# A room of its own for gathered token rows, and more filler products, in a two-layer mixture-of-experts encoder on Trainium2

## The chip, the cores and the metric

The kernel runs on 1 core of one Trainium2 chip, as one launch. The metric is the device time of one execution in microseconds (us); the time of the kernel before is the median of 3 runs.

## What is computed

Two layers, each an attention block and an expert block, over 512 tokens of width 1024, in float32. Here only the expert block matters ("expert choice": each of 16 experts takes the 64 tokens that like it best):

```python
h = rmsnorm(x, ffn_norm_g)
affinity = softmax(h @ w_router)                  # 512 x 16
gate, idx = top_k(affinity.T, 64)                 # per expert
xe = h[idx]                                       # 16 x 64 x 1024
a, u = xe @ w_gate, xe @ w_up                     # 1024 x 1408 per expert
y = (silu(a) * u) @ w_down                        # 1408 x 1024 per expert
x = x + scatter_add(y * gate, idx)
```

The weights of the experts are read once from HBM: 192 chunks of 1408 KB a layer.

## The kernel before, in words

A layer of `body` runs as attention (split by hand into units and placed by a table of due times), the output product with the router (the function `attention` returns the products, and the loop after it interleaves them with the router's work), and the expert block.

**Expert block.** The experts are taken in 8 pairs p = 0 to 7. Per pair there are 24 chunks of weights, numbered n = 24p + 8s + k: s = 0 is `w_gate`, s = 1 `w_up`, s = 2 `w_down`, and k is the slice of 128 rows. TensorE (PE) does the products of a chunk with the pair's 2 x 64 tokens (`L1302` for gate and up, 12 records a chunk; `L1347` for down, 14 a chunk on average), then the chunk's room is free. Between up and down stand SiLU on ScalarE (ACT, `L1327`), the product with up on VectorE (DVE, `L1328`) and PE transposes of the result (`L1336`).

**Rooms for chunks.** `load` and `bring` issue the chunk transfers on SyncE's (SP's) queue, in the order of n, and SP stands at each until its room is free. The first 17 chunks (table `ISSUE`) are brought in during attention, into rooms x0 to x11, y0, y1, "apart", the room of the hidden values ("hx") and a shared room "rows". Chunks 17 to 31 go into rooms that the table `AGAIN` names: x0 to x9 (17 to 26, once chunks 0 to 9 are used), y0, y1, x10, x11 (27 to 30, once 11, 12, 14, 15 are used), and x0 a second time (31, once 17 is used). From 32 on, two chunks go at once into a double room, in the order `DOUBLES = "bcdegfa"`: a is x0 and x1, b is x2 and x3, and so on to f; g is y0 and y1. So 32 and 33 wait in b for chunks 19 and 20.

**Rows of the tokens.** For pair p + 1 the 128 token rows are gathered from DRAM by an indirect DMA on GpSimd (POOL, `fetch_rows`, `L1248`), scaled by ACT (`L1249`) and transposed by PE (`L1256`) between up and down of pair p. They land in the room "rows", which for p = 0 first holds chunk 10. So the gather for pair 1 is issued behind chunk 10's products (`ROWS_AT = 2`: up, k = 2); all later ones behind gate's k = 6 (`MARK_AT`), as soon as `marks` has made the row numbers. ACT's instructions run in order: `L1249` stands ahead of the pair's SiLU.

**Router of the last token tile.** `stats`, `add_up`, `settle` and `best` make logits (`L958`), softmax (`L971` to `L977`), a transpose (`L981`), and eight rounds of maximum and replacement on DVE (`L1008`, `L1010`) for tile 3; then the threshold's transpose (`L1082`), ranks (`L1089` to `L1094`), and the first gathered tokens as products with a one-hot matrix (`L1205`), on which chunk 0's products wait. `warm` (`L998`) puts products of x with itself on PE there, whose results nobody reads: `WARM_A` (one 256 wide) before `stats`, `WARM_C` (two of 512) after `settle`, one of 512 in round 4 of `best(2)`, `WARM_P` (one of 512) before the first `L1205`. The scheduler may set them between other products.

`dynamic_dma_scratch_size=4096` reserves bytes of each partition for the descriptors of DMAs that POOL issues.

Of the kernel before, what the change touches and what calls it, by code (L numbers as in the profile page):

```python
# [11 lines left out]
F32 = mybir.dt.float32  # L12
# [17 lines left out]
FF = 1408  # L30
NJ = FF // P
CAP = 64
SLOT = 3072
RING = 3
ISSUE = [(16, "apart"), (0, "x0"), (1, "x1"), (4, "x4"), (11, "y0"), (2, "x2"), (3, "x3"), (10, "rows"), (5, "x5"), (6, "x6"), (7, "x7"), (9, "x9"), (8, "x8"), (13, "hx"), (14, "x10"), (15, "x11"), (12, "y1")]
AGAIN = ["x0", "x1", "x2", "x3", "x4", "x5", "x6", "x7", "x8", "x9", "y0", "y1", "x10", "x11", "x0"]
SINGLES = 32
DOUBLES = "bcdegfa"
GAP = 512
# [24 lines left out]
HALF_AT = 3  # L64
ROWS_AT = 2
END_ON = 'avavaa'
# [74 lines left out]
def body(ctx, tc, x_in, x_t, pos, w_in, w_uq, w_ukv, w_out, w_gate, w_up, w_down, gatt, gfin, params, consts, band, sel, out):  # L141
# [733 lines left out]
    for l in range(L):  # L875
        with ExitStack() as es:
# [196 lines left out]
            stats(t)  # L1073
            add_up(t)
            settle(t)
            warm(WARM_C)
# [20 lines left out]
            nc.vector.tensor_tensor(code, both[:, :, 0, :], both[:, :, 1, :], op=ALU.add)  # L1097
        with tc.tile_pool(name=f"fs{l}", bufs=1, reuse_waits="tile") as fs, tc.tile_pool(name=f"fw{l}", bufs=2, side="right", reuse_waits="tile") as fw, ExitStack() as late:
            early = ExitStack()
# [5 lines left out]

            def shared():

                return fs.tile([P, SLOT], F32, tag="rows", name=nm("shared"))

            def single(tag):  # L1110
                return fx.tile([P, 2 * FF], F32, tag=tag, name=nm("xslot"))

# [20 lines left out]

            near = {tag: single(tag) for tag in ("y0", "y1")}
            fx.tile([P, GAP], F32, tag="gap", name=nm("gap"))
            near.update({f"x{i}": single(f"x{i}") for i in range(12)})
            rooms = {}
            for n, tag in ISSUE:
                bring(n, xb.tile([P, 2 * FF], F32, tag="apart", name=nm("apart")) if tag == "apart" else wide() if tag == "hx" else shared()[:, : 2 * FF] if tag == "rows" else near[tag])

# [3 lines left out]
            def load(n):  # L1144

                if n not in kept:
                    if n < SINGLES:
                        bring(n, single(AGAIN[n - len(ISSUE)]))
                    else:
                        if n == SINGLES:  # L1150
                            early.close()
                            rooms["far"] = late.enter_context(tc.tile_pool(name=f"fd{l}", bufs=1, reuse_waits="tile"))
                            rooms["g"] = double("g")
                            rooms["far"].tile([P, GAP], F32, tag="gap", name=nm("gap"))
                            rooms.update({q: double(q) for q in "abcdef"})
# [86 lines left out]
            def fetch_rows(p):  # L1242

                if p > 0:
                    v, src = shared()[:, :D], xrow_d[l][:, :]
                else:
                    v, src = fw.tile([P, S], F32R, tag="oh", bufs=3, name=nm("rows")).bitcast(F32), xrow_d[l].rearrange("t (h d) -> (t h) d", h=2)
                nc.gpsimd.indirect_dma_start(v, None, src, bass.IndirectOffsetOnAxis(token[:, p : p + 1], 0))  # L1248
                nc.scalar.activation(v, v, AF.Copy, scale=scales[:, p : p + 1])  # L1249
                return v  # L1250
# [41 lines left out]
            for p in range(8):  # L1292
                acc, whole = [], {}
                ahead = [] if p < 7 else [(t, h) for t in range(NT - 1) for h in range(2)] if l == L - 1 else [(t, h) for h in range(2) for t in range(NT)][:6]
                for s, w in enumerate((w_gate, w_up)):
                    bs = [bank() for _ in cuts]
                    acc.append(bs)
                    for k in range(KD):
# [18 lines left out]
                        if w is w_gate and k == MARK_AT and p < 7:  # L1317
                            ohs[p + 1] = marks(p + 1)
                            if p > 0:
                                rows = fetch_rows(p + 1)  # L1320
                        if w is w_up and k == ROWS_AT and p == 0:
                            rows = fetch_rows(1)
                hx = wide()
# [164 lines left out]
```

## Time and profile before

| | |
|---|---|
| median of 3 runs (lowest, highest) | 1909.98 us (1909.73, 1911.14) |
| the profiled execution: its time, its span | 1910.87 us, 1909.1 us |
| PE, DVE, ACT, POOL busy | 1722.2 (90%), 703.6, 428.6, 206.1 us |
| mean granted TensorE clock | 0.981 |
| moved by DMA | 649.28 MB, mean 340 GB/s |
| chain that ended last | PE 48%, DMA 37%, DVE 9%, ACT 3% |

The profile cuts the span into 40 slices of 47.7 us; the expert block of layer 0 is slices 7 to 20, that of layer 1 slices 27 to 40. A granted clock of 1.00 is 2.4 GHz, 0.50 is 1.2 GHz. In a timeline row the first number is the start, the second the time from the first start to the last end of the instructions merged in it; in brackets stand the idle time before and what ended it.

### The profile page before, as it was taken

The page shows a single profiled execution, that of the slowest core. Times are in us where ns is not written, and L with a number is a line of the kernel's source. Part 1 is how long each engine was busy: PE and PEld are TensorE (multiplying, and loading weights), DVE is VectorE, ACT ScalarE, POOL GpSimd, SP SyncE. Part 2 cuts the span into 40 slices and gives each one's busy share as a digit, 9 for nine tenths or more (in the row PEclk, how much of TensorE's full clock was granted, in tenths as well). Part 3 has the DMA queues.
Part 4 walks back from the last instruction along what each step waited for, and adds up shares of the span by engine and source line. Part 5 has one row for each costly group of instructions (what it writes and reads, how often), then busy time and mean ns, then how long its engine had stood idle before and what let it go on. Part 6 is the DMA issues. An engine that isn't in the chain of part 4 may idle for free.

```text
span 1909.1 us, 21766 instructions
## 1 busy us (share of the span) xinstructions
PE 1722.2 (90%) x8798; PEld 895.9 (47%) x8798; DVE 703.6 (37%) x1470; ACT 428.6 (22%) x884; POOL 206.1 (11%) x232
## 2 busy tenths in 40 slices
PE   8999999999987878888899999989998878888887
PEld 6785675344332333333377756743443333333333
DVE  7868856111211112111188698541121112111112
ACT  5347941101000100000043589211100100000101
POOL 1324421000000000000023153210000000000000
PEclk9999998999999999999999999989999999999999
DMA  7874649989999999999948744798999999999996
GB/s 274 248 199 72 163 149 365 396 351 429 429 428 431 428 430 429 429 428 429 397 131 267 170 101 110 246 363 352 409 429 428 430 429 429 429 429 428 430 427 264
DMA packets 82579, 649.28 MB, mean 340 GB/s; under 512 B 8656, under 2 KB 25808, under 8 KB 53040
## 3 DMA queue, kind: packets, MB, share of 16 engines
q1 hardware_dynamic: 68288, 608.43, 78.7%
q0 software_dynamic: 12128, 35.54, 7.9%
q10 hardware_dynamic: 2064, 3.93, 0.6%
q8 instruction: 69, 1.13, 0.2%
q14 instruction: 30, 0.25, 0.0%
HBM read 619.17 MB, written 27.39 MB: 339 GB/s over the span
## 4 chain that ended last, share of the span: by engine, by line
PE 48%; DMA 37%; DVE 9%; ACT 3%; issue 1%; POOL 1%; SPq 0%; DVEq 0%; ACTq 0%; POOLq 0%
PE ps L1302 16%; DMA dslot<-in_w_up_dram 13%; DMA dslot<-in_w_gate_dram 13%; DMA dslot<-in_w_down_dram 9%; PE ps L1347 7%; PE ps L753 6%; PE ps L854 5%; PE ps L762 2%; PE ps L672 2%; PE ps L1277 2%; PE ps L655 2%; DVE sm L604 1%; PE ps L515 1%; ACT P L611 1%; DMA shared<-xrow_d,slots 1%
## 5 line engine op out<-in xcount | busy, mean ns | idle before, releaser
L1302 PE MATMUL ps<-dslot,xe 128*64 128x506 f32 (+1 forms) x2496 | 528.7, 575 | 87.3 <-DMA dslot<-in_w_up_dram 51.7
L1302 PEld LDWEIGHTS ps<-dslot,xe 128*64 128x64 f32 x2496 | 178.3, 139 | 425.8 <-issue 321.3
L1347 PE MATMUL ps<-dslot,hx 128*64 128x512 f32 (+3 forms) x1568 | 275.8, 504 | 46.1 <-DMA dslot<-in_w_down_dram 41.6
L1347 PEld LDWEIGHTS ps<-dslot,hx 128*64 128x64 f32 x1568 | 104.5, 137 | 209.4 <-issue 136.9
L1328 DVE TENSOR_TENSOR hx<-ps,hx 128x506 f32<-128x506 f32 (+1 forms) x48 | 43.4, 968 | 428.7 <-PE ps L1302 383.7
L1269 DVE SCALAR_TENSOR_TENSOR hx<-ps,gates,hx 128x512 fp32r<-128x512 f32 x32 | 22.5, 746 | 363.3 <-ACT hx L1268 363.3
L1268 ACT ACTIVATE hx<-ps,gates 128x512 fp32r<-128x512 f32 x32 | 20.3, 684 | 605.1 <-PE ps L1347 605.1
L753 PE MATMUL ps<-xh,w 128*128 128x512 f32 (+1 forms) x448 | 145.8, 405 | 3.1 <-ACT xh L363 1.4
L1279 DVE TENSOR_TENSOR x<-ps,x 128x512 f32<-128x512 f32 x112 | 69.5, 683 | 184.1 <-PE ps L1277 184.1
L1249 ACT ACTIVATE shared<-shared,slots 128x1024 f32<-128x1024 f32 x14 | 16.1, 1148 | 488.5 <-DMA shared<-xrow_d,slots 455.3
L611 ACT ACTIVATE P<-ps,sm 128x512 f32<-128x512 f32 x168 | 116.5, 704 | 32.1 <-DVE sm L604 30.8
L1248 POOL DMA_INDIRECT shared<-xrow_d,slots x14 | 13.2, 943 | 945.6 <-DVE oh L1239 887.6
L1302 PE MATMUL ps<-xslot,xe 128*64 128x506 f32 (+1 forms) x528 | 109.4, 560 | 3.9 <-DVE xe L1208 2.3
L753 PEld LDWEIGHTS ps<-xh,w 128*128 128x128 f32 (+1 forms) x448 | 84.2, 189 | 28.0 <-ACT xh L363 3.9
L753 PE MATMUL ps<-xl,w 128*128 128x512 f32 (+1 forms) x224 | 85.7, 393 | 0.0
L604 DVE TENSOR_REDUCE sm<-ps 128x1 f32<-128x512 f32 x120 | 78.7, 679 | 5.5 <-PE ps L589 4.6
L655 PE MATMUL ps<-ident,P 128*128 128x128 f32 x512 | 77.5, 274 | 2.0 <-ACT P L611 1.8
L663 ACT COPY pt<-ps 128x512 f32<-128x512 f32 x118 | 68.9, 604 | 25.9 <-PE ps L655 25.9
L655 PEld LDWEIGHTS ps<-ident,P 128*128 128x128 f32 x512 | 62.1, 140 | 25.6 <-ACT P L611 7.4
L1302 PEld LDWEIGHTS ps<-xslot,xe 128*64 128x64 f32 x528 | 35.8, 136 | 67.4 <-issue 59.6
L762 PE MATMUL ps<-w,xh 128*128 128x320 f32 (+1 forms) x256 | 62.2, 326 | 2.3 <-DVE w L340 2.3
L340 DVE TENSOR_TENSOR w<-slot,w 128x1024 fp32r<-128x1024 f32 (+4 forms) x46 | 53.7, 1170 | 26.3 <-ACT w L339 23.4
(290 smaller groups left out, 2088.6 us busy)
## 6 DMA issues: line engine op xcount, KB each, us to landing
dslot<-in_w_up_dram SPq DMA_DIRECT2D x56, 2816.0 KB, 42.6
dslot<-in_w_down_dram SPq DMA_DIRECT2D x48, 2816.0 KB, 41.0
dslot<-in_w_gate_dram SPq DMA_DIRECT2D x48, 2816.0 KB, 41.8
xslot<-in_w_gate_dram SPq DMA_DIRECT2D x32, 1408.0 KB, 9.5
xslot<-in_w_down_dram SPq DMA_DIRECT2D x14, 1408.0 KB, 9.0
dslot<-in_w_down_dram SPq DMA_DIRECT2D x14, 1408.0 KB, 36.1
xslot<-in_w_up_dram SPq DMA_DIRECT2D x12, 1408.0 KB, 10.0
slot<-in_w_in_dram SPq DMA_DIRECT2D x8, 1536.0 KB, 9.6
```

What stands on the lines that cost most here:

```text
L340: rest = lambda o=o, m=m, src=src: nc.vector.tensor_tensor(w[:, 1, :, o : o + m], src, w[:, 0, :, o : o + m].bitcast(F32), op=ALU.subtract)
L604: nc.vector.tensor_reduce(mn, ps, axis=AX.X, op=ALU.min)
L611: nc.scalar.activation(e, ps, AF.Exp, bias=mn, scale=-1.0, accum_out=lcol)
L655: nc.tensor.transpose(b[:, kc * P : (kc + 1) * P], e[:, kc * P : (kc + 1) * P], ident)
L663: nc.scalar.copy(dv, bv)
L753: nc.tensor.matmul(b[:m], w[:, passes[j][0], k, :m], passes[j][1](k), start=(n == 0), stop=(n == 3 * KD - 1))
L762: nc.tensor.matmul(acc[t][:, :m], xs, w[:, c, kk, :], start=(k == 0 and j == 0), stop=(k == KD - 1 and j == 2))
L854: nc.tensor.matmul(blocks[t][1 + h], o, w[h], start=(i == 0), stop=(i == 3 * KD - 1))
L1279: nc.vector.tensor_tensor(xv, b, xv, op=ALU.add)
L1302: tc.keep_in_program_order(nc.tensor.matmul(b[64 * i : 64 * i + 64, : qn * NJ], xe[:, k, 64 * i : 64 * i + 64], ws[i][:, q0 * NJ : (q0 + q ...
L1328: nc.vector.tensor_tensor(hv, u[:, : qn * NJ].rearrange("p (q j) -> p q j", j=NJ), hv, op=ALU.mult)
L1347: tc.keep_in_program_order(nc.tensor.matmul(bs[h][64 * i : 64 * i + 64, e % 512 : e % 512 + z - e], hT[:, j, 64 * i : 64 * i + 64], ws[i][ ...
```

## The change

The gathered rows get a room of their own in the pool `xb` (4 KB of each partition), and the scratch for POOL's DMA descriptors goes from 4096 to 1024 bytes. What was "rows" becomes an ordinary single room "s", which holds chunk 10 and then chunk 27; `AGAIN` no longer uses x0 twice. The double rooms are taken from a on. The gather for pair 1 stands where the others stand. `WARM_S` is new, `WARM_C` has three products, and round 6 of `best(2)` gets one of 256.

```diff
-ISSUE = [..., (10, "rows"), ...]
+ISSUE = [..., (10, "s"), ...]
-AGAIN = ["x0", "x1", "x2", "x3", "x4", "x5", "x6", "x7", "x8", "x9", "y0", "y1", "x10", "x11", "x0"]
+AGAIN = ["x0", "x1", "x2", "x3", "x4", "x5", "x6", "x7", "x8", "x9", "s", "y0", "y1", "x10", "x11"]
-DOUBLES = "bcdegfa"
+DOUBLES = "abcdegf"
-ROWS_AT = 2
-WARM_C = (512, 512)
+WARM_S = (512, 512)
+WARM_C = (512, 512, 512)
-WARM_B = {4: 512}
+WARM_B = {4: 512, 6: 256}
...
             add_up(t)
+            warm(WARM_S)
             settle(t)
             warm(WARM_C)
...
-            def shared():
-                return fs.tile([P, SLOT], F32, tag="rows", name=nm("shared"))
             def single(tag):
-                return fx.tile([P, 2 * FF], F32, tag=tag, name=nm("xslot"))
+                return fx.tile([P, SLOT if tag == "s" else 2 * FF], F32, tag=tag, name=nm("xslot"))[:, : 2 * FF]
...
                             rooms["far"] = late.enter_context(tc.tile_pool(name=f"fd{l}", bufs=1, reuse_waits="tile"))
+                            rooms["far"].tile([P, SLOT], F32, tag="s", name=nm("lay"))
...
                 if p > 0:
-                    v, src = shared()[:, :D], xrow_d[l][:, :]
+                    v, src = xb.tile([P, D], F32, tag="rows", name=nm("rows")), xrow_d[l][:, :]
...
                             ohs[p + 1] = marks(p + 1)
-                            if p > 0:
-                                rows = fetch_rows(p + 1)
-                        if w is w_up and k == ROWS_AT and p == 0:
-                            rows = fetch_rows(1)
+                            rows = fetch_rows(p + 1)
...
-    nc = _bacc.Bacc("TRN2", target_bir_lowering=False, num_devices=1, dynamic_dma_scratch_size=4096)
+    nc = _bacc.Bacc("TRN2", target_bir_lowering=False, num_devices=1, dynamic_dma_scratch_size=1024)
```

What moves on the engines. On POOL, at the start of layer 0's expert block, with the semaphores that each instruction waits for, the kernel before (`rows` is the gather for pair 0, `shared` those for pairs 1 and 2; DMAHW is a transfer of SP's queue):

```order
L1170 COPY pgf_2889<-a_all_2894 128x32x2 [waits DVE_49]
L1033 COPY spare_2898<-spare_2898 16x8 [waits DVE_49,Activation_49]
L1248 DMA rows_3353<-xrow_d_93,slots_3270 128x512 [waits DMASW2_49,DMASW1_49,DMASW3_49,DMASW0_49,DMASW4_49,DVE_49,Activation_49]
L1248 DMA shared_3460<-xrow_d_93,slots_3270 128x1024 [waits DMASW5_49,DMAHW6_49,DVE_49,PE_49]
L1248 DMA shared_3715<-xrow_d_93,slots_3270 128x1024 [waits DVE_49,DMASW6_49,PE_49,Activation_49]
```

and the changed one:

```order
L1169 COPY pgf_2889<-a_all_2894 128x32x2 [waits DVE_49]
L1033 COPY spare_2898<-spare_2898 16x8 [waits DVE_49,Activation_49]
L1247 DMA rows_3357<-xrow_d_93,slots_3274 128x512 [waits DMASW2_49,DMASW1_49,DMASW3_49,DMASW0_49,DMASW4_49,DVE_49,Activation_49]
L1247 DMA rows_3437<-xrow_d_93,slots_3274 128x1024 [waits DMASW5_49,DVE_49]
L1247 DMA rows_3719<-xrow_d_93,slots_3274 128x1024 [waits DVE_49,DMASW6_49,PE_49,Activation_49]
```

The gather for pair 1 no longer waits for PE (chunk 10's products) nor for a transfer of SP's; the others are as they were.

On PE, in layer 0's router for the last tile, from the transposes of x to the threshold's transpose, the kernel before:

```order
L949 MATMUL ps_3194<-ident,x 128x128 x4
L998 MATMUL ps_3200<-x 128x256
L958 MATMUL ps_3183<-pgf_2889,junk_2901 128x16 x4
L981 MATMUL ps_3217<-ident,a_all_2894 16x128
L998 MATMUL ps_3219<-x 128x512 x2
L996 MATMUL ps_3232<-spare_2898 8x8
L998 MATMUL ps_3232<-x 128x512
L1082 MATMUL ps_3242<-ident,xT_2903 128x16
```

and the changed one:

```order
L949 MATMUL ps_3194<-ident,x 128x128 x4
L998 MATMUL ps_3200<-x 128x256
L998 MATMUL ps_3217<-x 128x512
L958 MATMUL ps_3183<-pgf_2889,junk_2901 128x16 x4
L998 MATMUL ps_3217<-x 128x512
L981 MATMUL ps_3220<-ident,a_all_2894 16x128
L998 MATMUL ps_3222<-x 128x512 x3
L996 MATMUL ps_3236<-spare_2898 8x8
L998 MATMUL ps_3236<-x 128x512
L996 MATMUL ps_3243<-spare_2898 8x8
L998 MATMUL ps_3243<-x 128x256
L1083 MATMUL ps_3249<-ident,xT_2903 128x16
```

One of the two new products stands ahead of the logits `L958`, one behind them; a third and a narrow one come behind the softmax's transpose `L981`.

On DVE, in the same place, from the variance of the last tile on (`L971` to `L977` are its softmax, `L1008` and `L1010` on `aff` belong to tile 2, `L1008` on `ps` is the first maximum of the last tile), the kernel before:

```order
L1008 MAX spare_2898<-aff_2897 16x8
L971 TENSOR_REDUCE rr_3210<-ps_3183 128x1
L1010 MATCH_REPLACE aff_2897<-spare_2898,aff_2897 16x192
L972 TENSOR_TENSOR rr_3210<-rr_3210,rstds_2893 128x1
L1008 MAX spare_2898<-aff_2897 16x8
L1010 MATCH_REPLACE aff_2897<-spare_2898,aff_2897 16x192
L976 RECIPROCAL rr_3213<-rr_3213 128x1
L1008 MAX spare_2898<-aff_2897 16x8
L977 TENSOR_SCALAR a_all_2894<-a_all_2894,rr_3213 128x16
L1010 MATCH_REPLACE aff_2897<-spare_2898,aff_2897 16x192
L1008 MAX spare_2898<-ps_3217 16x8
L1008 MAX spare_2898<-aff_2897 16x8
```

and the changed one:

```order
L1008 MAX spare_2898<-aff_2897 16x8
L1010 MATCH_REPLACE aff_2897<-spare_2898,aff_2897 16x192
L971 TENSOR_REDUCE rr_3210<-ps_3183 128x1
L1008 MAX spare_2898<-aff_2897 16x8
L972 TENSOR_TENSOR rr_3210<-rr_3210,rstds_2893 128x1
L1010 MATCH_REPLACE aff_2897<-spare_2898,aff_2897 16x192
L1008 MAX spare_2898<-aff_2897 16x8
L976 RECIPROCAL rr_3213<-rr_3213 128x1
L1010 MATCH_REPLACE aff_2897<-spare_2898,aff_2897 16x192
L977 TENSOR_SCALAR a_all_2894<-a_all_2894,rr_3213 128x16
L1008 MAX spare_2898<-aff_2897 16x8
L1008 MAX spare_2898<-ps_3220 16x8
```

One replacement of tile 2 now stands ahead of `L971`, and tile 2's last maximum ahead of the first maximum of the last tile.

## Rows read from the trace of the kernel before

**Rows 1.** The page, GB/s moved in each of 40 slices.

```profile
GB/s 274 248 199 72 163 149 365 396 351 429 429 428 431 428 430 429 429 428 429 397 131 267 170 101 110 246 363 352 409 429 428 430 429 429 429 429 428 430 427 264
```

**Rows 2.** Windows, layer 0: stretch, length, PE, PEld, DVE, ACT, POOL busy (instructions), clock, DMA share, GB/s.

```profile
380.00:385.00 5.00, 5.00 (x18) 2.04 (x18) 1.61 (x3) 0.00 (x0) 0.00 (x0) 0.55 0.83 351
385.00:390.00 5.00, 5.00 (x38) 2.21 (x36) 0.00 (x0) 0.00 (x0) 0.00 (x0) 1.00 0.25 62
390.00:395.00 5.00, 5.00 (x32) 1.96 (x30) 0.00 (x0) 0.00 (x0) 0.00 (x0) 1.00 0.55 234
395.00:400.00 5.00, 5.00 (x34) 2.06 (x32) 0.00 (x0) 0.00 (x0) 0.00 (x0) 1.00 0.86 315
400.00:405.00 5.00, 5.00 (x28) 1.72 (x26) 1.41 (x2) 1.27 (x2) 0.00 (x0) 1.00 1.01 433
```

**Rows 3.** Windows, the same place in layer 1.

```profile
1325.00:1330.00 5.00, 5.00 (x28) 1.88 (x26) 0.00 (x0) 0.00 (x0) 0.00 (x0) 0.84 0.21 88
1330.00:1335.00 5.00, 5.00 (x32) 1.97 (x30) 0.00 (x0) 0.00 (x0) 0.00 (x0) 1.00 0.79 273
1335.00:1340.00 5.00, 5.00 (x34) 2.18 (x32) 0.00 (x0) 0.00 (x0) 0.00 (x0) 1.00 0.50 145
```

**Rows 4.** Timeline of SP's queue, layer 0: issues of chunks 30, 31, and 32 with 33.

```profile
374.45 0.33 SPq L1131 DMA_DIRECT2D xslot<-in_w_gate_dram  x1
...
387.77 0.33 SPq L1131 DMA_DIRECT2D xslot<-in_w_gate_dram  x1
...
394.86 0.33 SPq L1163 DMA_DIRECT2D dslot<-in_w_up_dram  x1
```

**Rows 5.** Timeline, layer 0, pair 0, from up to the hidden values.

```profile
362.88 0.97 POOL L1248 DMA_INDIRECT shared<-xrow_d,slots  x1 [28.93 <-PE ps L1302]
...
369.51 4.90 PE L1302 MATMUL ps<-xslot,xe 128*64 128x506 f32 x24
...
372.33 1.15 ACT L1249 ACTIVATE shared<-shared,slots 128x1024 f32<-128x1024 f32 x1 [30.87 <-DMA shared<-xrow_d,slots]
...
375.86 2.65 DVE L1328 TENSOR_TENSOR hx<-ps,hx 128x506 f32<-128x506 f32 x3 [22.15 <-ACT hx L1327]
```

**Rows 6.** Chain that ended last, layer 0: down of pair 0; up and down of pair 1.

```profile
381.17 20.74 PE ps L1347 x112
...
421.97 22.29 PE ps L1302 x112
448.92 19.13 PE ps L1347 x112
```

**Rows 7.** Timeline, layer 1, pair 0: end of up, start of down.

```profile
1311.44 4.90 PE L1302 MATMUL ps<-xslot,xe 128*64 128x506 f32 x24
...
1323.75 3.97 PE L1347 MATMUL ps<-apart,hx 128*64 128x512 f32 x12
```

**Rows 8.** Timeline of PE, layer 0, from the last tile's logits to chunk 1.

```profile
312.30 1.06 PE L958 MATMUL ps<-pgf,junk 128*128 128x16 f32 x8 [0.24 <-ACT junk L950]
...
315.38 0.27 PE L981 MATMUL ps<-ident,a_all 128*16 128x128 f32 x1 [2.02 <-DVE a_all L977]
...
322.81 2.06 PE L998 MATMUL ps<-x 128*128 128x512 f32 x2
...
324.66 1.95 PE L1205 MATMUL ps<-at,x 128*128 128x128 f32 x8
...
329.51 1.16 PE L1205 MATMUL ps<-at,x 128*128 128x128 f32 x8
```

**Rows 9.** Window of 1 us in the last tile's selection, layer 0.

```profile
316.00:317.00 1.00, 1.00 (x3) 0.45 (x2) 0.93 (x6) 0.00 (x0) 0.64 (x5) 0.62 0.91 379
```

**Rows 10.** Chain, end of layer 0: one float32 product 512 wide (two records).

```profile
933.86 1.05 PE ps L1283 x2
```

**Rows 11.** Timeline of POOL, attention of layer 0: the first four of nine loads of `st`.

```profile
136.57 2.19 POOL L524 DMA_DIRECT2D st<-bst_d  x4 [21.32 <-PE ps L762]
```

**Rows 12.** DMA issues: loads of `st`, KB each, median us to landing.

```profile
st<-bst_d POOLq DMA_DIRECT2D x40, 256.0 KB, 4.2
```

More of the change, by code (lines that the diff above doesn't have):

```diff
@@ L34 @@
 RING = 3
-ISSUE = [(16, "apart"), (0, "x0"), (1, "x1"), (4, "x4"), (11, "y0"), (2, "x2"), (3, "x3"), (10, "rows"), (5, "x5"), (6, "x6"), (7, "x7"), (9, "x9"), (8, "x8"), (13, "hx"), (14, "x10"), (15, "x11"), (12, "y1")]
-AGAIN = ["x0", "x1", "x2", "x3", "x4", "x5", "x6", "x7", "x8", "x9", "y0", "y1", "x10", "x11", "x0"]
+ISSUE = [(16, "apart"), (0, "x0"), (1, "x1"), (4, "x4"), (11, "y0"), (2, "x2"), (3, "x3"), (10, "s"), (5, "x5"), (6, "x6"), (7, "x7"), (9, "x9"), (8, "x8"), (13, "hx"), (14, "x10"), (15, "x11"), (12, "y1")]
+AGAIN = ["x0", "x1", "x2", "x3", "x4", "x5", "x6", "x7", "x8", "x9", "s", "y0", "y1", "x10", "x11"]
 SINGLES = 32
-DOUBLES = "bcdegfa"
+DOUBLES = "abcdegf"
 GAP = 512
@@ L1097, in body @@
             nc.vector.tensor_tensor(code, both[:, :, 0, :], both[:, :, 1, :], op=ALU.add)
-        with tc.tile_pool(name=f"fs{l}", bufs=1, reuse_waits="tile") as fs, tc.tile_pool(name=f"fw{l}", bufs=2, side="right", reuse_waits="tile") as fw, ExitStack() as late:
+        with tc.tile_pool(name=f"fw{l}", bufs=2, side="right", reuse_waits="tile") as fw, ExitStack() as late:
             early = ExitStack()
@@ L1132, in bring @@
                 kept[n] = v
-            near = {tag: single(tag) for tag in ("y0", "y1")}
+            near = {"s": fx.tile([P, SLOT], F32, tag="s", name=nm("slot"))[:, : 2 * FF]}
+            near.update({tag: single(tag) for tag in ("y0", "y1")})
             fx.tile([P, GAP], F32, tag="gap", name=nm("gap"))
@@ L1138, in body @@
             for n, tag in ISSUE:
-                bring(n, xb.tile([P, 2 * FF], F32, tag="apart", name=nm("apart")) if tag == "apart" else wide() if tag == "hx" else shared()[:, : 2 * FF] if tag == "rows" else near[tag])
+                bring(n, xb.tile([P, 2 * FF], F32, tag="apart", name=nm("apart")) if tag == "apart" else wide() if tag == "hx" else near[tag])
             def double(tag):
```

## The prediction, written before the result was known

> **What bounds the kernel now.** I read the 40 slices first, then windows of 5 us where their rates dip, then the timeline of SP, PE and ACT there. In the slices [rows 1], GB/s stands at 427 to 431 through nearly the whole expert block of both layers: its length is its bytes over that rate, plus whatever time the queue has nothing to carry. The dips inside the block are slices 7 to 9 (365, 396, 351) in layer 0 and 27 to 29 (363, 352, 409) in layer 1. So a layer gets shorter only if the stream of chunks starts earlier or stops less, and the reader should look for the stops.
>
> The windows show one clear stop. In layer 0 [rows 2] the rate falls to 351, 62, 234 and 315 GB/s from 380 to 400 us, while PE is busy all the time. Against 430 that is 79 + 368 + 196 + 115 = 758 GB/s short in windows of 5 us: 758 x 5 / 430 = 8.8 us of stream lost. In layer 1 [rows 3] it is 342 + 157 + 285 = 784, or 9.1 us. Why the queue ran dry is in SP's rows [rows 4]: chunk 30 is issued at 374.45, chunk 31 only at 387.77, chunks 32 and 33 only at 394.86. SP was standing for rooms: 31 for x0, which down's chunk 17 must leave; 32 for b, which chunks 19 and 20 must leave. Down of pair 0 begins only at 381.17.
>
> Down itself is late for another reason [rows 5]. Up ends at 369.51 + 4.90 = 374.41. The gather of pair 1's rows, issued behind chunk 10 at 362.88, has landed only when ACT starts scaling at 372.33; the activation table and SiLU queue behind it in ACT's order, and DVE's product starts at 375.86. Down starts 6.76 us after up's end. For pair 1, whose gather is early, it is 448.92 - (421.97 + 22.29) = 4.66 us, and its 112 products take 19.13 us against 20.74, which begin at a lower clock (0.55 in the first window of rows 2) [rows 6]. In layer 1 the same gap is 1323.75 - 1316.34 = 7.41 us [rows 7].
>
> **The change, part by part.** *Rooms.* Chunk 27 takes s, 28 to 30 move one room along, and 31 takes x11, free once chunk 15 is used. SP issued chunk 30 into that room at 374.45 before [rows 4], so 31 now goes then, and the queue has one chunk more: 1408 KB at 430 GB/s, 3.35 us. The queue ran dry at 380 + 5 x 351/430 = 384.1 in layer 0 [rows 2], so now at 387.4; in layer 1 at 1325 + 5 x 88/430 = 1326.0 [rows 3], now 1329.4. The next issue, 32 with 33, waits in room a for chunk 18 instead of 20.
>
> *Gather.* It is issued behind gate's k = 6, ten us earlier, and is back long before up's end, so ACT is free and down should start as for pair 1: at 374.41 + 4.66 = 379.07, and run at 19.13 / 112 = 0.171 us a product [rows 6]. Chunk 18 is then used after 42 products, at 379.07 + 7.17 = 386.24. From issue to a flowing stream it takes about 1.5 us: chunk 31 was issued at 387.77 [rows 4] and the window 385 to 390 moved 62 x 5 = 310 KB, or 0.7 us at full rate [rows 2], so it flowed from 389.3. The pair 32, 33 flows from 387.7, against dry at 387.4: 0.3 us lost instead of 8.8. Layer 1: 1316.34 + 4.66 + 7.17 + 1.5 = 1329.7, against 1329.4: 0.3 instead of 9.1. Behind that the double issues follow PE at 14 products x 0.171 x 2 = 4.8 us per two chunks, and the stream needs 6.7, so the queue grows. **Recovered: 8.5 + 8.8 = 17.3 us.**
>
> Bounds of this term: if only the rooms help and down starts and runs as before, chunk 18 is done at 387.77 + (394.86 - 387.77)/3 = 390.1, the pair flows from 391.6 and 4.2 us stay lost (4.6 in layer 1 by the same reckoning), leaving 9.1 recovered; if nothing stays lost it is 17.9. I take 17.3, because pair 1's rows are the same work with an early gather. The row traffic is the same bytes, moved 10 us earlier into a stream that loses nothing by it; the last room order leaves the layer's end alone, since the first loads of layer 1 wait behind the last chunks in the same queue anyway.
>
> *Products for the clock.* They work on the chain from the last tile's logits to chunk 0, on which the first freed rooms wait; a gain there moves the whole stream. Today PE idles 2.02 us ahead of L981 [rows 8], and just after it the granted clock passes from 1.00 to 0.50 (0.62 in the window where it falls) [rows 9]. One 512 wide product then takes 2.06 us, and the first eight records of L1205 1.95 instead of the 1.16 that they take at full clock [rows 8]. If the new products hold the clock, L1205 gives 0.8 us back. Against it, one of them stands ahead of L958: at full clock it takes 1.05 us [rows 10], PE had 0.24 idle there [rows 8], so the logits come 0.8 late; DVE gets about 0.35 back, since one replacement moves into that wait and no maximum of tile 2 stands inside the last tile's rounds. Net +0.35 us a layer, **0.7 in all**. Bounds: +1 a layer if the late logits are wholly covered; and if the clock falls all the same, three products at 2.06, then one, then a half one, 9.3 us, stand on PE from about 315.9, and the threshold's transpose comes near 325.2 instead of 321.6: 3.6 us lost a layer. I take the first because the pause of 2.02 is cut to about 1 us.
>
> *Scratch.* POOL's descriptors get 1024 bytes of a partition instead of 4096. No row shows a wait for descriptor room now. The densest use is nine loads of `st` in attention, the first four in 2.19 us [rows 11], each landing after 4.2 us [rows 12]. The Trainium skill (DMA: Bandwidth & Descriptors, SWDGE vs HWDGE vs iDMA) says that descriptors of GpSimd's DMAs are appended to rings in such a reserved piece of SBUF; with the 16 bytes a descriptor and the 9 per engine for a transfer of 128 rows that the page gives, 1024 bytes would hold seven transfers at once, an estimate, and the last two of nine would wait some 0.6 us. No run so far shows it. Without the page: the bound is nothing below, and above one load waiting for another, priced as a rival. I take 0, because these loads are for heads whose scores come later and POOL idles between the bursts.
>
> **The sum.** 17.3 + 0.7 = 18.0 us off the profiled execution's 1910.87, which lies 0.9 above the median: 1892.9 against it, and **1892.0** as a median of runs.
>
> **The rivals.**
> 1. *Only the rooms help* (something else holds ACT or PE before down, and the clock still falls): 9.1 recovered, so about 1901. Against it: no other wait stands ahead of SiLU for pair 1.
> 2. *The new products stand in the way*: 17.3 less 7.2, so about 1900. For it: PE takes its queue in order and half clock doubles each product. Against it: the busier PE should also bring the clock back sooner.
> 3. *The stream is not what sets the end*: the chunks come earlier and wait for PE, and the time moves under 2 us, near 1909. Against it: PE has 22.29 + 19.13 for 16 chunks of pair 1, about 2.6 us a chunk with 112 products for 8 at 19.13, below the 3.35 of the stream, and the rate is flat at 430 until the layer's end [rows 1].
> 4. *Slower, through the descriptors*: if 1024 bytes hold only one transfer, each of the nine loads of `st` waits for the one before: 9 x 4.2 = 38 us where 5 are spent now, 33 us a layer on POOL, 66 in both; less 18, the kernel ends near 1958. It is slower as soon as POOL's stalls put over 9 us a layer on the heads' scores. For it: nothing in the trace bounds what the smaller scratch does. Against it: the loads are spread in groups with pauses, and one transfer a time would be a quarter of a room that today shows no wait at all.
>
> **How the numbers follow.** Forecast 0.74, rival 1 0.08, rival 2 0.08, rival 3 0.04, rival 4 0.06. The forecast's own ends: 17.9 + 2 = 19.9 gives 1890; 16 - 1 = 15 gives 1895. The range of 8 in 10 goes on to the near edge of rivals 1 and 2 and a little below the forecast: 1888.5 to 1900. A measurement here tells 0.2%, 3.8 us, from no change; forecast and rivals 1 and 2 are faster by more (0.90), rival 3 is the same (0.04), rival 4 slower (0.06).
>
> **What would show it.** In the changed profile: SP issues chunk 31 near 375 and 32 near 386 in layer 0; no window between 380 and 400 below 400 GB/s; ACT scales pair 1's rows near 363 and DVE's product with up starts near 374; down starts within 5 us of up's end, at clock 1.00; the window around 317 shows 1.00; nine loads of `st` end within a us of where they end now. Wrong it would be if the dry stretch only moves (another stop in the first 100 us of the block), if a product at 2 us stands ahead of the threshold's transpose, or if POOL's loads spread out.

## The result and the profile after

The changed kernel takes **1891.38 us** (median of 4 runs, 1891.07 to 1892.73) beside 1910.56 for the kernel before on the same chip: a ratio of 0.9902, with a 95% interval of 0.989 to 0.9914. (The ratios are estimated from the single runs and are not the quotients of the medians; the differences in us below are between medians.) That is 19.2 us less, against 18.0 forecast (1892.0; range 1888.5 to 1900). The profiled execution took 1891.34 us, its span is 1889.6, and its mean granted clock 0.989 where before it was 0.981.

First the slices of the page, as in [rows 1]:

```profile
GB/s 276 251 196 77 165 145 357 395 430 428 430 427 431 428 429 429 429 428 430 393 125 271 176 89 124 220 362 423 429 429 430 429 428 430 429 428 429 430 427 263
```

Slice 9 was 351 and is 430, slice 28 was 352 and is 423. The dip in slices 7 and 8 (357, 395) has stayed, as has that in 27. The windows of the stretches that had been dry, first layer 0, then layer 1 (columns as in [rows 2]):

```profile
380.00:385.00 5.00, 5.00 (x34) 2.19 (x32) 0.00 (x0) 0.00 (x0) 0.00 (x0) 1.00 0.98 410
385.00:390.00 5.00, 5.00 (x30) 1.83 (x28) 0.00 (x0) 0.00 (x0) 0.00 (x0) 1.00 1.08 460
390.00:395.00 5.00, 5.00 (x34) 2.23 (x32) 0.00 (x0) 0.00 (x0) 0.00 (x0) 1.00 1.00 428
395.00:400.00 5.00, 5.00 (x28) 1.78 (x26) 1.41 (x2) 1.26 (x2) 0.00 (x0) 1.00 1.01 433
...
1310.00:1315.00 5.00, 5.00 (x34) 2.23 (x32) 0.61 (x2) 0.00 (x0) 0.00 (x0) 1.00 1.02 428
1315.00:1320.00 5.00, 5.00 (x30) 1.83 (x28) 0.00 (x0) 0.00 (x0) 0.00 (x0) 1.00 1.06 436
1320.00:1325.00 5.00, 5.00 (x34) 2.20 (x32) 0.00 (x0) 0.00 (x0) 0.00 (x0) 1.00 1.00 430
```

Beside [rows 2, 3], where the rate fell to 62 and 88, no window is under 400. (One of 410 and one of 460 stand beside each other: their mean is 435, so nothing is lost.) SP's issues of chunk 31 and of 32 with 33, beside [rows 4]:

```profile
373.12 0.33 SPq L1128 DMA_DIRECT2D xslot<-in_w_gate_dram  x1
...
383.60 0.33 SPq L1162 DMA_DIRECT2D dslot<-in_w_up_dram  x1
```

Chunk 31 goes 14.65 us earlier than before, 32 with 33 goes 11.26 earlier. And what PE, ACT and DVE do meanwhile (timeline, layer 0, pair 0, beside [rows 5]; some lines have moved by 1 to 4):

```profile
352.21 0.96 POOL L1247 DMA_INDIRECT rows<-xrow_d,slots  x1 [19.48 <-DVE slots L1229]
...
362.24 1.15 ACT L1248 ACTIVATE rows<-rows,slots 128x1024 f32<-128x1024 f32 x1 [22.37 <-DMA rows<-xrow_d,slots]
...
368.18 4.90 PE L1301 MATMUL ps<-xslot,xe 128*64 128x506 f32 x24
368.40 2.63 ACT L1323 ACTIVATE hx<-ps 128x506 f32<-128x506 f32 x3 [3.71 <-PE ps L1301]
...
371.67 2.73 DVE L1324 TENSOR_TENSOR hx<-ps,hx 128x506 f32<-128x506 f32 x3 [19.28 <-PE ps L1301]
...
376.24 2.58 PE L1343 MATMUL ps<-apart,hx 128*64 128x512 f32 x12 [0.37 <-DVE hx L1333]
```

The gather's rows are scaled at 362.24 instead of 372.33, SiLU runs at 368.40 while up is still at work, and down starts 376.24 - (368.18 + 4.90) = 3.16 us behind up's end, where it was 6.76. In layer 1 the same gap went from 7.41 [rows 7] to 3.17. Down's 112 products take 19.13 us in the chain of waits now, not 20.74 [rows 6].

PE's timeline in the last tile's selection, beside [rows 8]:

```profile
312.40 0.96 PE L958 MATMUL ps<-pgf,junk 128*128 128x16 f32 x8
313.21 1.10 PE L998 MATMUL ps<-x 128*128 128x512 f32 x2
315.29 0.28 PE L981 MATMUL ps<-ident,a_all 128*16 128x128 f32 x1 [0.98 <-DVE a_all L977]
...
322.36 1.10 PE L998 MATMUL ps<-x 128*128 128x512 f32 x2
324.06 1.23 PE L1204 MATMUL ps<-at,x 128*128 128x128 f32 x8 [0.60 <-ACT at L1193]
```

The pause ahead of L981 is 0.98 us instead of 2.02, the window from 316 to 317 shows a clock of 1.00 where it was 0.62 [rows 9], and the first eight records of the `at` product take 1.23 us, not 1.95. PE also waits there now (0.60, for ACT), where before it came last.

**Where the time went.** From the last tile's turning (the last L949 ahead of chunk 0) to chunk 0 it is 325.67 - 310.61 = 15.06 us (before: 327.00 - 310.96 = 16.04), and in layer 1 1259.03 - 1243.98 = 15.05 (before 1268.93 - 1252.89 = 16.04): 2.0 us less in both. From chunk 0 of layer 0 to that turning in layer 1 it is 918.31 us (925.89), and from chunk 0 of layer 1 to the span's end 630.57 (640.17): 7.6 and 9.6, 17.2 in the streams (the first of the two stretches holds attention of layer 1 as well). The remaining 0.35 is attention of layer 0. How much of the 2.0 is the new products' is told with the runs on them: the stage's length also varies where no instruction of it differs.

### The profile page after: what moved, and what is told of

Read it like the earlier page. It is cut to its first block, busy times and chain, and to the rows that moved or that the text cites. A ratio compares the mean times of both kernels' runs of the same rounds, so it can differ in the third digit from the quotient of the medians.

```text
span 1889.6 us, 21800 instructions
## 1 busy us (share of the span) xinstructions
PE 1714.8 (91%) x8818; PEld 894.5 (47%) x8818; DVE 703.9 (37%) x1470; ACT 428.4 (23%) x884; POOL 205.4 (11%) x232
## 4 chain that ended last, share of the span: by engine, by line
PE 46%; DMA 38%; DVE 9%; ACT 3%; issue 1%; SPq 1%; POOL 1%; DVEq 0%; POOLq 0%; ACTq 0%
PE ps L1301 16%; DMA dslot<-in_w_up_dram 14%; DMA dslot<-in_w_down_dram 13%; DMA dslot<-in_w_gate_dram 11%; PE ps L1343 6%; PE ps L753 5%; PE ps L854 5%; PE ps L762 2%; PE ps L672 2%; PE ps L1276 2%; PE ps L655 2%; PE ps L515 1%; DVE sm L604 1%; ACT P L611 1%; DVE P L639 1%
## 5 line engine op out<-in xcount | busy, mean ns | idle before, releaser
L753 PE MATMUL ps<-xh,w 128*128 128x512 f32 (+1 forms) x448 | 144.1, 401 | 2.7 <-ACT xh L357 1.3
L1248 ACT ACTIVATE rows<-rows,slots 128x1024 f32<-128x1024 f32 (+1 forms) x16 | 17.5, 1095 | 498.9 <-DMA rows<-xrow_d,slots 498.9
L1247 POOL DMA_INDIRECT rows<-xrow_d,slots x16 | 15.4, 961 | 957.3 <-DVE oh L1238 888.6
L753 PEld LDWEIGHTS ps<-xh,w 128*128 128x128 f32 (+1 forms) x448 | 83.1, 186 | 26.9 <-ACT xh L363 3.2
L753 PE MATMUL ps<-xl,w 128*128 128x512 f32 (+1 forms) x224 | 85.7, 393 | 0.0
```

The lines of the kernel that those rows point to most:

```text
L753: nc.tensor.matmul(b[:m], w[:, passes[j][0], k, :m], passes[j][1](k), start=(n == 0), stop=(n == 3 * KD - 1))
```

## The experiments

They ran on chips on which the kernel before took 1910.20, 1911.28 and 1911.03 us (medians of 15, 17 and 9 runs). So what is compared below is each kernel's difference to the kernel before beside it. For the changed kernel that is -19.2 above, and in a second measurement:

**The changed kernel again**, with no edit.

> The changed kernel as it stands, beside the next two on one chip, so that a difference of a few us between kernels is not one between chips. Expected: a ratio of 0.990 to 0.9915 to the kernel before, and 2 us or more between single runs.

Measured: 1891.94 us (1890.07 to 1894.76), ratio 0.9906 [0.989, 0.9921], -19.1. It repeats, and differences under 2 us between kernels are not told apart here by the times.

### Rooms and gather, each without the other

**The rooms undone.** Gather and products stay:

```diff
-AGAIN = [..., "x8", "x9", "s", "y0", "y1", "x10", "x11"]
-DOUBLES = "abcdegf"
+AGAIN = [..., "x8", "x9", "y0", "y1", "x10", "x11", "x0"]
+DOUBLES = "bcdegfa"
```

> The changed kernel with the old order of rooms (x0 used twice, doubles from b on; s holds chunk 10 alone); gather, products and scratch as changed. By the sum chunk 31 waits for chunk 17 and 32 for chunk 20 again, both some 3.6 us earlier than before, so 8.8 - 3.6 = about 5 us a layer stay dry: 1900 to 1902 us. If the gather's wait was the whole of it, it comes within 2 us of the changed kernel.

Measured: 1897.12 us (1896.68 to 1898.01), ratio 0.9927 [0.9914, 0.9941], -13.1. SP's issues of 31 and of 32 with 33, and the windows, layer 0:

```profile
381.58 0.33 SPq L1128 DMA_DIRECT2D xslot<-in_w_gate_dram  x1
388.67 0.33 SPq L1162 DMA_DIRECT2D dslot<-in_w_up_dram  x1
```

```profile
385.00:390.00 5.00, 5.00 (x30) 1.82 (x28) 0.00 (x0) 0.00 (x0) 0.00 (x0) 1.00 0.63 223
390.00:395.00 5.00, 5.00 (x34) 2.18 (x32) 0.00 (x0) 0.00 (x0) 0.00 (x0) 1.00 0.89 369
```

The stream is short by (37 + 207 + 61) x 5 / 430 = 3.5 us (37 from the window before, 393 GB/s). Six us dearer than the changed kernel, and less dear than expected: with down starting 3.16 us behind up's end, even the old rooms come free early enough to save more than half.

**The gather's call moved back**, rooms and products stay:

```diff
                         if w is w_gate and k == MARK_AT and p < 7:
                             ohs[p + 1] = marks(p + 1)
-                            rows = fetch_rows(p + 1)
+                            if p > 0:
+                                rows = fetch_rows(p + 1)
+                        if w is w_up and k == 2 and p == 0:
+                            rows = fetch_rows(1)
```

> The changed kernel with the gather for pair 1 put back behind up's k = 2 of pair 0; rooms, products and scratch as changed. The sum has it that down then starts 2 to 2.7 us later and partly at the lower clock, so chunk 18 frees its room some 3.6 us late and about 4 us a layer stay dry: 1897 to 1900 us. If the rooms alone fill the stream, it comes within 2 us of the changed kernel.

Measured: 1892.61 us (1891.46 to 1895.47), ratio 0.9907 [0.9893, 0.9921], -17.6: not told apart from the changed kernel. But the run did not do what it was made for. POOL's row shows the gather where it was:

```profile
352.32 0.97 POOL L1247 DMA_INDIRECT rows<-xrow_d,slots  x1 [19.48 <-DVE slots L1229]
```

Before, the gather waited for PE, which had to be done with chunk 10 in the shared room ([rows 5]: released by PE, 362.88). With a tile of its own it waits only for its row numbers, and POOL has nothing else in its queue there, so the place of the call in the program sets nothing. It shows that the gather came early through its room, not through the place of its call. The late gather itself was left to the next run.

**The row numbers late**, so that the gather is late; rooms and products stay. For pair 0, the numbers of pair 1 are made behind up's k = 2, and PE is held to that place:

```diff
-                        if w is w_gate and k == MARK_AT and p < 7:
-                            ohs[p + 1] = marks(p + 1)
+                        if (w is w_gate and k == MARK_AT and 0 < p < 7) or (w is w_up and k == 2 and p == 0):
+                            ohs[p + 1] = marks(p + 1, pin=p == 0)
                             rows = fetch_rows(p + 1)
```

> The changed kernel, but the row numbers of pair 1, and so the gather of its rows, are only made behind up's k = 2 (as before the change) instead of gate's k = 6, and PE is held to that place; rooms and products stay. Theory of the prediction (the gather's place is worth something of its own): the gather is issued near 363 and lands near 372 instead of 362, ACT scales ahead of SiLU, down of pair 0 starts 1.5 to 3 us later and with PE idle 6 us or more at a lower clock, chunk 18 leaves room a later by 2 to 4 us, and 2 to 4 us a layer stay dry: 1895.5 to 1900. Rival (the rooms alone carry the gain, the gather only had to be moved for the rooms' sake): 32 and 33 are issued later, but the queue holds enough by then: within 2 us of the changed kernel, 1891 to 1893.5.

Measured: 1899.41 us (1897.61 to 1902.67), ratio 0.9939 [0.9927, 0.9951], -11.9. Timeline, layer 0 (POOL, ACT, down's start on PE and the issue of 32 with 33), and the windows around:

```profile
361.68 0.96 POOL L1247 DMA_INDIRECT rows<-xrow_d,slots  x1 [28.93 <-DVE slots L1229]
371.74 1.15 ACT L1248 ACTIVATE rows<-rows,slots 128x1024 f32<-128x1024 f32 x1 [31.92 <-DMA rows<-xrow_d,slots]
372.91 1.28 ACT L1323 ACT_TABLE_LOAD   x1
374.20 2.54 ACT L1323 ACTIVATE hx<-ps 128x506 f32<-128x506 f32 x3
...
380.50 2.94 PE L1343 MATMUL ps<-apart,hx 128*64 128x512 f32 x12
...
388.21 0.33 SPq L1162 DMA_DIRECT2D dslot<-in_w_up_dram  x1
```

```profile
375.00:380.00 5.00, 2.04 (x10) 2.05 (x11) 4.57 (x7) 1.75 (x3) 0.00 (x0) 0.78 1.00 421
...
385.00:390.00 5.00, 5.00 (x34) 2.11 (x32) 0.00 (x0) 0.00 (x0) 0.00 (x0) 1.00 0.41 126
390.00:395.00 5.00, 5.00 (x32) 1.96 (x30) 0.00 (x0) 0.00 (x0) 0.00 (x0) 1.00 0.91 387
```

Chunk 0 starts at 325.68 here, as in the changed kernel, so the rows can be laid on each other: the gather is issued 9.5 us later, ACT scales 9.5 later, PE falls idle and its clock to 0.78, 32 with 33 goes 4.6 us later, and the stream is short for about 4 us. Up ends where it did (368.19 + 4.90 = 373.09, in the changed kernel 373.08), so holding PE to that place costs nothing by then; 4.3 of the 4.6 us are down's later start (380.50, was 376.24). So with the new rooms the early gather is worth another 7 us, and the rival, that the rooms alone carry the gain, has fallen.

**Only the first double undone**; chunk 31 keeps its new room x11:

```diff
-DOUBLES = "abcdegf"
+DOUBLES = "bcdegfa"
```

> The changed kernel with one part of the rooms undone: the double rooms are again taken from b on, so chunks 32 and 33 wait for chunk 20 and not 18; chunk 31 keeps its new room x11. Theory (31's room and the first double each give their part): 31 is issued near 373 as in the changed kernel, 32 only near 388.3 instead of 383.6; the queue, which has work until about 387.5 with 31 in it, is dry for 1 to 3 us a layer: 1893 to 1897. Rival (31's room is the whole gain of the rooms): unchanged within 1.2 us, 1891 to 1892.6. Rival (the first double is the whole gain): as with all rooms old, 1896.5 to 1898.

Measured: 1901.85 us (1899.90 to 1902.81), ratio 0.9944 [0.9932, 0.9957], -9.4: dearer than with all rooms old. Of that, 2.7 us lie ahead of the experts (chunk 0 starts at 328.39 and not 325.67; the last section tells of it). The time lies above every range of the expectation; what separates its cases is the trace. SP's issues and the windows:

```profile
375.84 0.33 SPq L1128 DMA_DIRECT2D xslot<-in_w_gate_dram  x1
391.04 0.33 SPq L1162 DMA_DIRECT2D dslot<-in_w_up_dram  x1
```

```profile
385.00:390.00 5.00, 5.00 (x30) 1.94 (x28) 0.00 (x0) 0.00 (x0) 0.00 (x0) 1.00 0.77 324
390.00:395.00 5.00, 5.00 (x34) 2.17 (x32) 0.00 (x0) 0.00 (x0) 0.00 (x0) 1.00 0.65 225
```

Counted from chunk 0, 31 is issued at 47.45, as early as in the changed kernel (47.45), and 32 at 62.65, as late as with all rooms old (62.66). The stretch is short by 3.7 us, no less than the 3.5 with all rooms old. So an early chunk 31 alone gives nothing: it lets the queue run dry behind 31 instead of ahead of it. What counts is when 32 with 33 goes, and that is the second rival's case. Chunk 31's move matters only because it empties x0, of which room a is made: that lets the doubles begin with a, which waits for chunk 18, and not with b, which waits for 20.

The four cases, all with the new products, as differences in us to the kernel before (neither part is the run "only the products" below):

| | gather late | gather early |
|---|---|---|
| rooms old | -1.9 | -13.1 |
| rooms new | -11.9 | -19.2 |

Each part alone gives 10 to 11 us, both 17.3. They work on the same issue, that of 32 with 33: counted from chunk 0 it goes at 67.86 before (394.86 - 327.00), at 62.66 with only the gather early, at 62.53 with only the rooms new, at 57.93 with both. Some 5 us come from each, and the stream stops for 8.8, 3.5, 4.1 and 0 us in layer 0, and by the same reckoning for 9.1, 3.7, 4.9 and 0 in layer 1. Once it no longer stops, an earlier issue saves nothing more: of the 9.9 us that both together bring in layer 0, 8.8 were needed. So the gains don't add: in the dry time of both layers the two alone save 10.7 and 8.9 us, both together 17.9. (By the times it is 11.2, 10.0 and 17.3; the rest of that difference is within the spread of the runs.)

### The products for the clock

**Without the new products**, the rest as changed:

```diff
-WARM_S = (512, 512)
-WARM_C = (512, 512, 512)
-WARM_B = {4: 512, 6: 256}
+WARM_S = ()
+WARM_C = (512, 512)
+WARM_B = {4: 512}
```

> The changed kernel without its new products for the clock (WARM_S empty, WARM_C two, no product in round 6); rooms, gather and scratch as changed. If the rooms and the gather carry nearly all of it, as the sum has it, this comes about 1 to 2 us a layer behind the changed kernel, at 1893 to 1895 us, and the clock falls behind the softmax of the last tile as it did before, while the stream stays full from 380 to 400 us. If the products are what keeps the stream full (the clock of the first chunks), it comes at 1900 or later.

Measured: 1893.08 us (1892.86 to 1895.65), ratio 0.991 [0.9894, 0.9926], -17.1, so the products give 2.0 beside the second measurement of the changed kernel by the medians, and 0.8 to 1.5 by the ratios (0.991 beside 0.9906 and 0.9902). By the times alone that is not told from nothing. In its trace the clock falls, and the first eight records of the `at` product take 1.67 us in layer 0 and 1.98 in layer 1; the stream stays full (no window from 380 to 400 under 420 GB/s).

**Only the products**, on the kernel before:

```diff
-WARM_C = (512, 512)
-WARM_B = {4: 512}
+WARM_S = (512, 512)
+WARM_C = (512, 512, 512)
+WARM_B = {4: 512, 6: 256}
...
             add_up(t)
+            warm(WARM_S)
             settle(t)
```

> The kernel before with the new products alone. If their worth is the earlier start of chunk 0, this gains 1 to 1.4 us a layer: 1907 to 1908.5 us, with the stream as dry as before at 380 to 400 us. If the earlier start is lost in the dry stretch behind it, it stays at 1910.

Measured: 1908.26 us (1905.85 to 1911.71, 11 runs), ratio 0.999 [0.9981, 0.9999], -1.9. The interval just leaves out 1.

How much of this is the products' is better read from the stage itself, from the last tile's turning to chunk 0, over all traces of this document. In the three kernels without the new products it took 16.04 and 16.04 us (before; layers 0 and 1), 15.64 and 15.77 (the run above) and 15.02 and 15.75 (only the smaller scratch, below), 15.7 on average. In the nine traces with all of the new products it took 15.04 to 15.06 us in 16 of 18 cases, and 15.77 and 15.76 in the other two, 15.1 on average. The `at` product of layer 0 in two of them, first this run, with all new products, then only the smaller scratch, with none:

```profile
324.11 1.94 PE L1207 MATMUL ps<-at,x 128*128 128x128 f32 x8 [0.60 <-ACT at L1196]
```

```profile
326.20 1.23 PE L1205 MATMUL ps<-at,x 128*128 128x128 f32 x8 [0.59 <-ACT at L1194]
```

In the first the granted clock fell, to 0.57 from 324 to 326 us, though every new product stood in its place; in the second it had fallen behind the softmax's transpose and was back at 1.00 in time. So the products don't make the stage shorter than it can be without them. They make the short case the usual one, which is worth 0.6 us a layer on average, 1.2 in all; the 2.0 above is the difference to one trace, in which both layers had 16.04.

**Only the two ahead of L981**, the rest as changed:

```diff
-WARM_C = (512, 512, 512)
-WARM_B = {4: 512, 6: 256}
+WARM_C = (512, 512)
+WARM_B = {4: 512}
```

> The changed kernel with only the two products ahead of the threshold's transpose (WARM_S); the third one behind it and the half one of WARM_B are taken out. Theory (the fall of the clock came from the pause ahead of L981, which these two fill): the granted clock stays 1.00 at 316 to 317 and the first records of the at product take about 1.2 us: 1891 to 1892.3, as with all of them. Rival (the later pauses matter as well): the clock falls behind one of them, and the time is near that without any new product, 1892.6 to 1893.5.

Measured: 1895.47 us (1894.37 to 1896.38), ratio 0.9913 [0.99, 0.9926], -15.8. As above, some 2.7 us of it lie ahead of this stage (L949 at 313.34 instead of 310.61). From there to chunk 0 it is 329.06 - 313.34 = 15.72 us, against 15.06 with all products and 326.39 - 310.75 = 15.64 without. Two windows of 2 us (columns as in [rows 2]) and PE's rows behind them:

```profile
322.00:324.00 2.00, 0.80 (x2) 0.00 (x0) 1.72 (x9) 0.00 (x0) 0.00 (x0) 1.00 0.94 284
324.00:326.00 2.00, 1.46 (x10) 1.08 (x11) 0.89 (x5) 0.00 (x0) 0.00 (x0) 0.69 0.98 406
```

```profile
324.09 0.22 PE L1083 MATMUL ps<-ident,xT 16*128 16x16 f32 x1 [1.30 <-DVE xT L1081]
...
325.24 2.06 PE L998 MATMUL ps<-x 128*128 128x512 f32 x2
327.08 1.59 PE L1204 MATMUL ps<-at,x 128*128 128x128 f32 x8
```

The clock holds through L981 and falls a few us later, behind pauses of 1.53 and 1.30 us, and the `at` product takes 1.59 (1.23 in the changed kernel, 1.95 before). Layer 1's stage takes 16.14 us. With the later products missing the stage is as long as without any, so the rival is borne out: here part of the fill gives nothing, and a fill that reaches to the end of the stage mostly, not always, holds the clock.

### The scratch

**Only the smaller scratch**, on the kernel before:

```diff
-    nc = _bacc.Bacc("TRN2", ..., dynamic_dma_scratch_size=4096)
+    nc = _bacc.Bacc("TRN2", ..., dynamic_dma_scratch_size=1024)
```

> The kernel before with 1024 instead of 4096 bytes of scratch for GpSimd's DMA descriptors and nothing else changed. Theory of the prediction: no difference, 1909 to 1911.5, and the nine loads of st end where they ended. Rival 4 of the prediction: each of the nine waits for the one before, and the time goes up by tens of us, to 1930 or more.

Measured: 1911.61 us (1910.36 to 1913.04, 11 runs), ratio 0.9999 [0.999, 1.0008]. A cost of more than 2 us is ruled out, and none is seen.

**Half of that**, on the changed kernel:

```diff
-    nc = _bacc.Bacc("TRN2", ..., dynamic_dma_scratch_size=1024)
+    nc = _bacc.Bacc("TRN2", ..., dynamic_dma_scratch_size=512)
```

> The changed kernel with 512 bytes of scratch for GpSimd's DMA descriptors instead of 1024. Theory (the scratch sets nothing here at this size either): the time of the changed kernel within 1 us, the nine loads of st in their bursts. Rival (1024 is just enough): the later loads of a burst wait for earlier ones, the bursts spread by microseconds on POOL, and the time goes up by 2 us or more.

Measured: 1893.58 us (1893.11 to 1897.51), ratio 0.9918 [0.9904, 0.9931], -17.5. POOL's loads of `st` in layer 0, first with 1024 bytes (changed kernel), then with 512:

```profile
136.26 2.30 POOL L524 DMA_DIRECT2D st<-bst_d  x4 [21.34 <-PE ps L762]
139.17 2.16 POOL L524 DMA_DIRECT2D st<-bst_d  x4 [0.61 <-PE ps L655]
```

```profile
136.31 1.68 POOL L524 DMA_DIRECT2D st<-bst_d  x3 [21.44 <-PE ps L762]
140.11 0.54 POOL L524 DMA_DIRECT2D st<-bst_d  x1 [2.11 <-issue]
141.45 0.54 POOL L524 DMA_DIRECT2D st<-bst_d  x1 [0.80 <-issue]
...
145.67 0.54 POOL L524 DMA_DIRECT2D st<-bst_d  x1 [0.94 <-issue]
```

The burst has eight loads (the prediction counted nine). With 512 bytes POOL issues three and then stands 2.11 us, about until the first would have landed (the median landing is 3.9 us in this trace, 136.31 + 3.9 = 140.2), and ahead of each of the next four 0.55 to 1.10 us: the burst ends at 146.21 instead of 141.33. The profile names no releaser for these waits ("issue"), and they are absent with 1024 bytes, where the scratch is all that differs. So there is a limit, and here it lay at three loads for 512 bytes. The time goes up by 1.6 us, with intervals that overlap, and not through this burst: chunk 0 of layer 0 starts at 325.68, as in the changed kernel (325.67). Of the 1.6 us, 0.7 are layer 1's selection, one of the two cases above in which the clock fell all the same (15.76 us); where the rest comes from was not followed.

### A version that might beat both

What is left of the dips is the stretch from 325 to 345 (310 GB/s on average), where SP stands for rooms and PE takes 4.05 us a chunk, with pauses for DVE's copies (changed kernel, timeline of PE):

```profile
338.17 2.58 PE L1301 MATMUL ps<-xslot,xe 128*64 128x506 f32 x12 [0.38 <-DVE xe L1207]
...
342.13 4.95 PE L1301 MATMUL ps<-xslot,xe 128*64 128x506 f32 x24 [0.78 <-DVE xe L1256]
```

The edit puts the next operand's products ahead of the last third of a chunk's own:

```diff
                         for b, (q0, qn) in zip(bs, cuts):
+                            if w is w_gate and p == 0 and q0 == cuts[2][0]:
+                                for f in EARLY[k + 1] if k + 1 < len(EARLY) else ():
+                                    fill(xg, xe, *f, pin=True)
+                                if k == HALF_AT:
+                                    turn_rows(rows, xe, 4, 4)
                             for i in range(2):
...
-                            for f in EARLY[k + 1] if k + 1 < len(EARLY) else ():
-                                fill(xg, xe, *f, pin=True)
...
-                            if k == HALF_AT:
-                                turn_rows(rows, xe, 4, 4)
```

> A version that may beat both: the changed kernel, but in gate of pair 0 the products that make the next chunk's operand (L1204, and the turning of the fetched rows, L1255) stand ahead of the last third of the running chunk's products and not behind it, so that DVE's copy of their result lies beside PE's work. What is left of the dips, 284 to 329 GB/s from 325 to 345 us, comes from gate's first chunks taking 4.05 us each on PE where the stream brings one in 3.35, and of these 4.05 PE idles 0.38 three times and 0.78 once. Theory (those pauses set when rooms come free there): chunk 4 starts 1.3 to 1.7 us earlier after chunk 0 in each layer, and the time falls by 2.5 to 3.5 us, to a ratio 0.0013 to 0.0018 under that of the changed kernel. Rival (the stop is elsewhere, or the operands' copies take their time from the next wait): within 1 us of the changed kernel.

Measured: 1891.13 us (1890.97 to 1893.04), ratio 0.9901 [0.9886, 0.9916], 0.8 us under the changed kernel beside it. In its timeline the pauses are gone from chunk 1 on:

```profile
336.45 1.16 PE L1204 MATMUL ps<-at,x 128*128 128x128 f32 x8
337.54 2.58 PE L1306 MATMUL ps<-xslot,xe 128*64 128x396 f32 x12
```

Chunk 6 starts 346.96 - 326.26 = 20.70 us after chunk 0, where it was 347.81 - 325.89 = 21.92 on the same chip. But of these 1.2 us layer 0 keeps 0.7 up to layer 1's chunk 0 (932.63 us against 933.34), and layer 1 none up to the end (630.5 against 629.9). So this is no better than the changed kernel by what can be measured; the rival stands, and where the 1.2 us go was not followed.

## Why the prediction was right, point by point

- **The bound** was as read: the stream of chunks sets a layer's length, and the missing bytes in the dips of [rows 2, 3] were lost time. Of 17.3 us forecast for the stops, 17.2 show in the two stretches behind chunk 0 (7.6 and 9.6, forecast 8.5 and 8.8).
- **31 near 375, 32 near 386**: 373.12 and 383.60. Of the 2.6 us that 32 came earlier than forecast, 1.3 are chunk 0's earlier start, and 1.5 the gap ahead of down, 3.16 and not 4.66. The gap was taken from pair 1, "the same work with an early gather", and that was right; the reading of it was not. The chain's row for up, 421.97 with 22.29 [rows 6], ends at 444.26 because the chain passes there from PE to DVE, not because up is done. PE's timeline and DVE's first product, pair 1 of the kernel before:

```profile
443.64 2.11 PE L1302 MATMUL ps<-dslot,xe 128*64 128x506 f32 x10
444.35 2.72 DVE L1328 TENSOR_TENSOR hx<-ps,hx 128x506 f32<-128x506 f32 x3 [21.66 <-PE ps L1302]
```

Up ends at 443.64 + 2.11 = 445.75 and down starts at 448.92, so the gap was 3.17 us there already, and DVE starts 1.40 us before up's end, as it now does in pair 0 (371.67 and 373.08). Read from the timeline, pair 1 would have given pair 0's new gap exactly. The 1.5 us bought little, as only 0.3 were still lost by the forecast.
- **The step on 31's room was wrongly argued**, without harm to the sum. The text gave it "one chunk more: 1408 KB at 430 GB/s, 3.35 us". The run with only the first double undone shows that it gives nothing where 32 stays late. The 3.35 us were right only together with 32's earlier room, which chunk 31's move makes possible.
- **Rival 1 (only the rooms help)** was priced at 9.1 us recovered. The run with the late gather is this case: -11.9, less 1.9 for the products, 10.0. Its place in the argument was right; the trace of the changed kernel shows that it didn't happen.
- **The products** are the term whose size is the least sure: "net +0.35 us a layer, 0.7 in all" beside 2.0 against the one trace of the kernel before, 1.2 on average over all traces, and 0.8 to 2.0 by runs whose intervals reach some 3 us to either side. Two parts of the step were off. The logits were to come 0.8 late, by the product's 1.05 ahead of L958; they came 0.45 late (312.40 against 312.30, with attention 0.35 earlier). And the gain was counted at L1205 alone, 0.8, though the product ahead of it also went from 2.06 to 1.10, so that PE was no longer last there: it now waits 0.60 for ACT's `at`. Rival 2 (they stand in the way, 3.6 us lost a layer) needed the clock to fall all the same; in the changed kernel it stayed at 1.00 from 310 to 330. In the two cases in which it did fall, it fell only behind the threshold's transpose, so no product of 2 us stood ahead of that, and the stage was no longer than before. What the step left out is that the fall itself varies between stages with the same instructions.
- **Rival 3** (the stream does not set the end) fell with the result.
- **The scratch** was taken at 0: the run with it alone says 0.9999. The Trainium skill's figures (DMA: Bandwidth & Descriptors, The descriptor swizzle and Terms: 9 descriptors of 16 bytes for each engine) gave an estimate of seven transfers in 1024 bytes; by the same reckoning 512 would hold three, and three is what POOL issued in a row there. Of the 0.6 us that "the last two of nine" loads were to wait by it, the trace with 1024 shows none among the eight that there are: the one pause in the burst, 0.61 us, ends with a product of PE. Rival 4 (1024 bytes hold one transfer, 33 us a layer) fell with that: half of them hold three.
- **The layer's end** was to stay as it was. A product at the start of layer 1 (`L753`) comes 9.1 us earlier (953.56, was 962.66), and down of layer 0 ends 9.1 earlier too.

## What to carry to other kernels

Where a queue of transfers runs dry behind several late rooms in a row, find the issue behind which the stream flows again, and price every edit by how much earlier that one issue goes: an earlier transfer ahead of it only moves the dry stretch. Two edits that pull at the same issue don't add, so price each with and without the other. Whether an instruction comes earlier is read from what releases it (its room, its numbers), not from where its call stands in the program. When a stage ends is read from the engine's own timeline; a row of the chain of waits ends where the chain goes on to another engine, here 1.5 us early. And a gain of 1 us in a stage whose clock moves is read from many traces, not from one before and one after.

## What was not expected of the hardware

The granted clock in the first 30 us differed between traces whose instructions there are the same. PE is idle for 3.1 us ahead of L380 in each of these two, and the windows of 5 us behind that read, for the changed kernel and then for the one with only the first double undone (columns as in [rows 2]):

```profile
25.00:30.00 5.00, 4.80 (x23) 3.53 (x24) 1.86 (x5) 4.76 (x12) 0.14 (x1) 1.00 1.07 363
```

```profile
25.00:30.00 5.00, 4.57 (x13) 3.38 (x14) 2.08 (x5) 4.76 (x12) 0.38 (x1) 0.50 1.06 356
```

At 0.50, 13 records instead of 23 fit into the stretch, and chunk 0 comes 2.7 us later (328.39 against 325.67). The kernel with only WARM_S has the same. Only the changed kernel has two traces, so whether the other runs of these two lost the 2.7 us as well is not shown. In the kernel before, for one, and in those without the new products, with the late numbers and with the old rooms, the clock was lower at another place instead, 0.83 on average from 10 to 20 us. So it was in the second measurement of the changed kernel (0.79 and 0.86 in its two windows of 5 us from 10 to 20), whose first trace reads 1.00 there: the same kernel shows both, so this doesn't belong to an edit. No edit touches anything there; the runs don't say what decides it. It is one more reason to compare stages, from one marker to the next, and not spans, when a few us are in question.
